# A list scheduler's cost tables: durations and hand-over times by engine pair, and GpSimd and SBUF-to-SBUF VectorE operations apart in the plan

## The chip, the cores and the metric

The kernel runs on one core of a Trainium2 chip. Its time is the device time of one execution in microseconds (us), the median of the runs shown. Five engines work side by side, each through its own list of instructions in order, and wait for one another by semaphores: TensorE (PE, matmuls), VectorE (DVE), ScalarE (ACT), GpSimd (POOL), and SyncE (SP), which issues the DMAs.

## What is computed

The reference is a chain of three transformer layers on 512 tokens of width 1024 in fp32, with 256 tokens of memory. Cut to what matters:

```python
def reference(x, mem, positions, ...):
    mem_n = rmsnorm(mem)
    for i in range(2):                      # first block
        hn = rmsnorm(x)
        mix, q_cross = mla_mixer(hn) if i == 0 else swa_mixer(hn)
        cross = memory_cross_attention(q_cross, mem_n, w_mem_kv[i])
        x = x + concat([mix, cross]) @ w_o[i]
        x = x + squared_relu_mlp(rmsnorm(x), w_up[i], w_down[i])
    x = rmsnorm(x)
    ...                                     # second block, one layer
    a_b, a_c, a_x, q, kc, vc, ksl, vsl, kwn, vwn, g_nsa, g_merge = split(rmsnorm(x) @ w_in)
    y_a = a_b * causal_dwconv(a_c * a_x)
    y_b = nsa(rope(rmsnorm(q)), compressed, selected and window keys and values, gates)
    x = x + (gm_a * (y_a @ w_a_out) + gm_b * (y_b @ w_b_out)) @ w_o
    g, u = split(rmsnorm(x) @ w_ffn_in)
    return x + (silu(causal_dwconv(g) + b) * u) @ w_ffn_out
```

MLA has 12 heads on low-rank queries and keys (`c_q`, `c_kv`, each with a norm of its own, nq and nkv) and a rotated key that all heads share (kr). SWA has 12 heads with a window of 128 tokens, NSA 8 heads with three branches each (compressed, selected, window).

## The kernel before

The activations stay in SBUF transposed, as 8 tiles of 128 features by 512 tokens (`x`). Every dense product is made to fp32 accuracy from three matmuls: a weight chunk (128x512, 256 KB) is loaded by SyncE into one of 4 `raw` buffers, ScalarE rounds it to `h`, and DVE takes the rest, `l = raw - h` (`load_chunk`). For the chunks of the MLA, SWA and first NSA projections GpSimd makes `l` instead (`pool_chunk`). The activation is split in the same way into two `pgr` tiles, and h times both halves and l times the first are summed in PSUM. There are 8 `h` and 8 `l` buffers, and PSUM has 3 banks for dense products (`psd`), 2 for scores (`pss`), 2 for transposes and broadcasts (`pst`) and 1 for values (`pso`). `pgf` are fp32 work tiles of 128x512, `sm` tiles of a few columns.

A norm takes the sums of squares over features with 128x1 matmuls into `pst`, makes the inverse root on DVE with 15 operations on 128x4 elements (`rstd_cols`, `rsqrt`), puts it on the diagonal of four 128x128 blocks, and multiplies these with a matrix of ones on PE, so that every partition has the row; ScalarE copies it to SBUF (`bcast_rows`). The dense products of a normed activation start from x itself, and the row is multiplied in when `psd` is evacuated. n0 is the norm ahead of MLA, nq and nkv are those inside.

The program doesn't run in the order in which it is written. All engine calls are recorded first (`Trace.add`), each as an `Op` with its cost by `_op_cost`, its inputs and its tiles. `Trace.schedule` then makes a plan of the whole kernel: at each step it takes the operation that can start earliest by the plan, and among several on one engine the first by the program's order (with a bias by hand for some groups). An operation can start when its inputs are visible, its engine is free and a buffer is free for each new tile. Visible means the producer's end plus `AFTER` of the producer's engine plus `BEFORE` of the consumer's (`AFTER = {"PE": 197.0, "DVE": 128.0, "ACT": 132.0, "POOL": 75.0, "SP": 2000.0}`). The order in which the plan takes them is the order of each engine's instructions and of the buffers (`emit`); the planned times themselves are used for nothing else. On the chip each engine runs its list as fast as semaphores allow. Since all calls go out from one line of `emit`, that line (L415) stands in every row of the profile, and the names of tiles tell the places apart.

## Time and profile before

| | |
|---|---|
| median of 3 runs | 1916.19 us (1915.88 to 1916.23) |
| span of the profiled execution | 1914.9 us |
| PE busy | 1856.5 us (97%) |
| weight loads of PE | 1527.4 us (80%) |
| DVE busy | 1169.7 us (61%) |
| ACT busy | 835.5 us (44%) |
| POOL busy | 388.9 us (20%) |

The span runs from the first to the last instruction of one profiled execution; the runs' times are 1.3 us longer on the median. A row of the timeline gives start and duration of an instruction (or of several alike in a row, with "x" and their count), the engine, what it writes and reads, and in brackets how long the engine had been idle ahead of it and which engine's result ended that. The durations of matmuls in a row overlap. The clock in the stretches is the share of TensorE's full 2.4 GHz that was granted; 0.5 is its lower level, 1.2 GHz.

In order of time the stages are: memory projections (12 to 43 us), the projections and heads of MLA (to 240), output and MLP (to 640), SWA (to 762), output and MLP (to 1145), the second block's projections and sparse attention (to 1340), and its output and FFN.

### The profile page before, as it was taken

The numbers are of one execution on the slowest core, as the hardware profiler recorded it, in microseconds if no ns is written. First come the engines' busy times: TensorE is split into PE (matmuls) and PEld (weight loads), VectorE is DVE, ScalarE is ACT, GpSimd is POOL, SyncE is SP. The second block draws the span as 40 slices with busy tenths as digits, with TensorE's granted clock in tenths as the row PEclk, the third lists the DMA queues.
The fourth block names the chain that finished last, engine by engine and source line by source line (L and its number), as shares of the span: only waits on it lengthen the run. The fifth ranks groups of instructions, "written<-read, shape, count | busy, mean of one in ns | idle before, by whom it ended". The sixth has DMA issues, their size and how long they took to land.

```text
span 1914.9 us, 25100 instructions
## 1 busy us (share of the span) xinstructions
PE 1856.5 (97%) x8749; PEld 1527.4 (80%) x8749; DVE 1169.7 (61%) x2268; ACT 835.5 (44%) x1674; POOL 388.9 (20%) x431
## 2 busy tenths in 40 slices
PE   6789999999999998999999999999999999999999
PEld 6567688888888876888888887778888888888887
DVE  8588875444446688654444356777755567774652
ACT  7378644332424677443323243447633333332321
POOL 4454320000001354100000040455300122110100
PEclk9899999999999999999999999899999999999999
DMA  6211133333333210333333322311133233333332
GB/s 214 79 49 50 45 94 104 95 99 95 98 99 95 78 56 17 99 105 95 98 98 95 99 81 58 105 45 45 56 94 99 89 93 105 94 99 99 94 99 76
DMA packets 92150, 166.98 MB, mean 87 GB/s; under 512 B 10612, under 2 KB 12408, under 8 KB 92024
## 3 DMA queue, kind: packets, MB, share of 16 engines
q1 hardware_dynamic: 92024, 165.40, 28.8%
q8 instruction: 68, 1.11, 0.2%
q14 instruction: 58, 0.48, 0.1%
HBM read 161.68 MB, written 2.10 MB: 86 GB/s over the span
## 4 chain that ended last, share of the span: by engine, by line
PE 86%; DVE 7%; ACT 3%; issue 2%; POOL 1%; DMA 1%; SPq 0%; DVEq 0%; POOLq 0%; ACTq 0%
PE psd L415 77%; PE pst L415 3%; DVE pgf L415 3%; PE pso L415 3%; PE pss L415 3%; DVE pgr L415 2%; DVE sm L415 1%; ACT pgf L415 1%; ACT pgr L415 1%; POOL pgf L415 1%; DVE l L415 1%; ACT h L415 1%; DMA raw<-w 0%; DVE x L415 0%; DMA pgf<-memT 0%
## 5 line engine op out<-in xcount | busy, mean ns | idle before, releaser
L415 PE MATMUL psd<-pgr,h 128*128 128x512 f32 (+2 forms) x4622 | 1448.8, 393 | 16.2 <-ACT h L415 11.6
L415 PEld LDWEIGHTS psd<-pgr,h 128*128 128x128 f32 (+1 forms) x4622 | 867.4, 189 | 196.0 <-ACT h L415 11.6
L415 PE MATMUL psd<-pgr,l 128*128 128x512 f32 (+2 forms) x2311 | 905.8, 392 | 0.8 <-DVE l L415 0.8
L415 DVE TENSOR_TENSOR l<-raw,h 128x512 fp32r<-128x512 f32 (+1 forms) x536 | 419.4, 785 | 453.9 <-ACT h L415 451.9
L415 ACT CAST h<-raw 128x512 fp32r<-128x512 f32 (+2 forms) x601 | 368.6, 616 | 700.8 <-PE psd L415 618.5
L415 PEld LDWEIGHTS psd<-pgr,l 128*128 128x128 f32 (+1 forms) x2311 | 436.5, 189 | 91.2 <-issue 3.5
L415 POOL TENSOR_TENSOR pgf<-pgf,pgf 128x512 f32<-128x512 f32 (+1 forms) x106 | 142.3, 1345 | 1078.8 <-ACT pgf L415 770.9
L415 DVE TENSOR_TENSOR pgr<-pgf,pgr 128x512 fp32r<-128x512 f32 (+4 forms) x184 | 130.4, 710 | 14.5 <-ACT pgr L415 9.5
L415 ACT CAST pgr<-pgf 128x512 fp32r<-128x512 f32 (+4 forms) x184 | 108.3, 591 | 58.3 <-POOL pgf L415 31.6
L415 ACT ACTIVATE pgf<-pgf 128x512 f32<-128x512 f32 (+2 forms) x125 | 74.9, 602 | 116.4 <-DVE pgf L415 113.2
L415 DVE TENSOR_TENSOR pgf<-psd,pgf 128x512 f32<-128x512 f32 (+2 forms) x102 | 66.9, 657 | 75.3 <-PE psd L415 73.8
L415 POOL TENSOR_TENSOR l<-raw,h 128x512 fp32r<-128x512 f32 (+1 forms) x65 | 88.8, 1377 | 89.5 <-ACT h L415 68.0
L415 PE MATMUL pso<-pgr,pgr 128*128 128x512 f32 (+3 forms) x368 | 90.6, 341 | 4.2 <-DVE pgf L415 1.8
L415 DVE TENSOR_TENSOR pgr<-pst,pgr 128x512 fp32r<-128x512 f32 (+1 forms) x126 | 74.1, 610 | 15.2 <-ACT pgr L415 14.6
L415 POOL TENSOR_SCALAR pgf<-pgf,sm 128x256 f32<-128x256 f32 (+3 forms) x128 | 70.1, 566 | 65.5 <-DVE sm L415 49.6
L415 PE MATMUL pst<-cstt,pgf 128*128 128x128 f32 x436 | 77.7, 277 | 2.6 <-POOL pgf L415 1.5
L415 ACT CAST pgr<-pst 128x512 fp32r<-128x512 f32 (+1 forms) x126 | 63.3, 529 | 28.2 <-PE pst L415 26.8
L415 PE MATMUL pss<-pgr,pgr 128*128 128x256 f32 (+4 forms) x320 | 69.1, 315 | 6.1 <-DVE sm L415 4.0
L415 PEld LDWEIGHTS pso<-pgr,pgr 128*128 128x128 f32 x368 | 58.4, 189 | 19.6 <-ACT pgr L415 7.3
L415 DVE CUSTOM_DVE_ANT_0 pgf<-pss,cmask 128x256 f32<-128x256 f32 (+3 forms) x144 | 65.7, 469 | 12.9 <-PE pss L415 10.8
L415 ACT ACTIVATE pgf<-pgf,sm 128x256 f32<-128x256 f32 (+3 forms) x128 | 65.9, 516 | 16.0 <-DVE sm L415 15.5
L415 PEld LDWEIGHTS pst<-cstt,pgf 128*128 128x128 f32 x436 | 52.7, 140 | 20.5 <-POOL pgf L415 8.3
(115 smaller groups left out, 1122.8 us busy)
## 6 DMA issues: line engine op xcount, KB each, us to landing
raw<-w SPq DMA_DIRECT2D x588, 256.0 KB, 2.6
x<-xT SPq DMA_DIRECT2D x8, 256.0 KB, 5.6
out<-x SPq DMA_DIRECT2D x8, 256.0 KB, 2.0
pgf<-pgf SPq DMA_DIRECT2D x24, 64.0 KB, 2.0
pgf<-aux SPq DMA_DIRECT2D x5, 256.0 KB, 2.7
pgf<-memT SPq DMA_DIRECT2D x4, 256.0 KB, 4.4
raw<-w SPq DMA_DIRECT2D x7, 140.0 KB, 2.1
raw<-w SPq DMA_DIRECT2D x4, 192.0 KB, 2.5
```

The lines of the kernel that those rows point to most:

```text
L415: getattr(getattr(nc, names[o.eng]), o.method)(*[r(x) for x in o.args], **{k: r(v) for k, v in o.kw.items()})
```

## The change

Only the planner changes. The costs in `_op_cost` get other constants (matmuls in fp32r cost their columns plus 32 at 2.4 per ns with a floor of 105 ns, a DMA at least 420 ns of its queue, ScalarE 95 ns more for each operand of one column, a sum taken along costs 75 to 110, and a result of one column on DVE costs 70). The two lists of hand-over times become one table by pair of engines, and 100 ns are added where the result is the operand that PE loads as weights. And in the plan an operation of GpSimd (other than memset), or one of DVE of four kinds that has no PSUM operand, starts only after the last such operation of the other of the two engines has ended. Recorded operations, tiles and their counts stay; their order and the buffers they get may differ.

```diff
--- before.py
+++ after.py
@@ -298,12 +298,30 @@
 
 
 ENGINES = {"tensor": "PE", "vector": "DVE", "scalar": "ACT", "gpsimd": "POOL", "sync": "SP"}
-AFTER = {"PE": 197.0, "DVE": 128.0, "ACT": 132.0, "POOL": 75.0, "SP": 2000.0}
-BEFORE = {"PE": 135.0, "DVE": 0.0, "ACT": 0.0, "POOL": 45.0, "SP": 0.0}
+LAT = {
+    "PE": {"PE": 0.0, "DVE": 211.0, "ACT": 205.0, "POOL": 310.0, "SP": 250.0},
+    "DVE": {"PE": 137.0, "DVE": 126.0, "ACT": 122.0, "POOL": 190.0, "SP": 150.0},
+    "ACT": {"PE": 155.0, "DVE": 140.0, "ACT": 138.0, "POOL": 240.0, "SP": 150.0},
+    "POOL": {"PE": 140.0, "DVE": 150.0, "ACT": 101.0, "POOL": 215.0, "SP": 150.0},
+    "SP": {"PE": 1950.0, "DVE": 1950.0, "ACT": 1950.0, "POOL": 1950.0, "SP": 1950.0},
+}
+LOAD_WEIGHTS = 100.0
+
+
+PORT = ("DVE", "POOL")
+
+
+def _uses_port(o):
+
+    if o.eng == "POOL":
+        return o.method != "memset"
+    if o.eng != "DVE" or any(v.tile.whole for v in o.reads + o.writes):
+        return False
+    return o.method in ("tensor_tensor", "scalar_tensor_tensor", "tensor_scalar", "tensor_copy")
 
 
 class Op:
-    __slots__ = ("i", "eng", "method", "args", "kw", "reads", "writes", "cost", "preds", "succs", "tiles",
+    __slots__ = ("port", "i", "eng", "method", "args", "kw", "reads", "writes", "cost", "preds", "succs", "tiles",
                  "prio", "bias", "npred", "est", "end")
 
 
@@ -318,21 +336,26 @@
     if eng == "PE":
         if method == "transpose":
             return 109.0
-        m, k = _free(args[1]) / 1.2, _free(args[2]) * 0.4167
-        return (max(2 * m, 4 * k) if args[2].dtype == FT else max(m, k)) + 2.5
+        k = _free(args[2])
+        if args[2].dtype == FT:
+            return 2 * max(111.0, (2 * k + 8) / 2.4)
+        return max(105.0, (k + 32) / 2.4)
     if eng == "SP":
-        return 60.0 + n * writes[0].shape[0] * 4 / 340.0
+        return max(420.0, n * writes[0].shape[0] * 4 / 400.0)
+    scalars = [x for x in list(args[2:4]) + [kw.get(k) for k in ("scalar", "bias", "scale")]
+               if isinstance(x, View) and _free(x) == 1]
     if eng == "ACT":
-        return 0.833 * n + (52 if psum else 93) + (220 if accum else 0)
-    scalars = [x for x in list(args[2:4]) + [kw.get("scalar")] if isinstance(x, View) and _free(x) == 1]
+        return 0.833 * n + (52 if psum else 93) + 95 * len(scalars) + (110 if accum else 0)
     if eng == "POOL":
         if method == "memset":
             return 0.833 * n + 60
         if method == "tensor_tensor":
-            return 2.2 * n + 100
-        return 0.833 * n + 160 + 64 * len(scalars)
+            return 2.2 * n + 150
+        return 0.833 * n + 185 + 64 * len(scalars)
     n = max([n] + [_free(v) for v in reads if method == "tensor_reduce"])
-    extra = 68 + (60 if scalars or accum else 0)
+    extra = 68 + (60 if scalars else 0) + (75 if accum else 0)
+    if n == 1:
+        return 70.0
     if method in ("tensor_copy", "tensor_scalar", "memset") and not psum:
         return 0.521 * n + extra
     return 1.042 * n + extra
@@ -403,6 +426,7 @@
         out_costs = writes if writes else [v for v in reads]
         o.cost = _op_cost(eng, method, args, kw, reads, out_costs)
         o.eng = eng
+        o.port = _uses_port(o)
         self.ops.append(o)
 
     def emit(self, tc, order):
@@ -446,6 +470,8 @@
         done = np.zeros(n, bool)
         cur = 0
         engt = {e: 0.0 for e in ENGINES.values()}
+        portt = {e: 0.0 for e in PORT}
+        other = {"DVE": "POOL", "POOL": "DVE"}
         ready = {e: [] for e in engt}
         future = {e: [] for e in engt}
         parked = {}
@@ -483,7 +509,8 @@
                     heapq.heappop(q)
                     offer(o)
                     continue
-                return (engt[e] if r else f[0][0]), o.i
+                at = engt[e] if r else f[0][0]
+                return (max(at, portt[other[e]]) if o.port else at), o.i
 
         for o in ops:
             if o.npred == 0:
@@ -504,15 +531,23 @@
             o.est = st
             o.end = st + o.cost
             engt[e] = o.end
+            if o.port:
+                portt[e] = o.end
             order.append(i)
             done[i] = True
             while cur < n and done[cur]:
                 cur += 1
-            vis = o.end + AFTER[e]
+            lat = LAT[e]
+            vis = o.end + (1950.0 if e == "SP" else 130.0)
             for j in o.succs:
                 s = ops[j]
                 s.npred -= 1
-                s.est = max(s.est, vis + BEFORE[s.eng] if (s.eng != e or e != "PE") else st)
+                if s.eng == "PE" and e != "PE":
+                    own = {id(v.tile) for v in o.writes}
+                    t = o.end + lat["PE"] + (LOAD_WEIGHTS if id(s.args[1].tile) in own else 0.0)
+                else:
+                    t = o.end + lat[s.eng] if (s.eng != e or e != "PE") else st
+                s.est = max(s.est, t)
                 if s.npred == 0:
                     offer(s)
             for t in o.tiles:
```

Three places of the order that follows. Numbers behind a tile's name are buffers.

PE at the broadcast of n0, before (51 to 64 us): `pst` from `ones` is the broadcast, the `psd` rows are MLA's first projections, which read x and weights alone.

```order
L415 MATMUL psd_279<-pgr_318,h_166 128x512
L415 MATMUL psd_279<-pgr_332,h_166 128x512
L415 MATMUL psd_279<-pgr_318,l_178 128x512
L415 MATMUL psd_173<-pgr_318,h_176 128x512
L415 MATMUL pst_359<-pgf_330,ones_72 128x512
L415 MATMUL psd_173<-pgr_332,h_176 128x512
L415 MATMUL psd_173<-pgr_318,l_189 128x512
L415 MATMUL psd_180<-pgr_348,h_191 128x512
L415 MATMUL psd_180<-pgr_361,h_191 128x512
```

The same place after the change.

```order
L439 MATMUL psd_306<-pgr_341,h_273 128x512
L439 MATMUL psd_306<-pgr_492,h_273 128x512
L439 MATMUL psd_306<-pgr_341,l_293 128x512
L439 MATMUL psd_172<-pgr_341,h_282 128x512
L439 MATMUL psd_172<-pgr_492,h_282 128x512
L439 MATMUL psd_172<-pgr_341,l_302 128x512
L439 MATMUL pst_401<-pgf_242,ones_72 128x512
L439 MATMUL psd_179<-pgr_189,h_309 128x512
L439 MATMUL psd_179<-pgr_267,h_309 128x512
```

In the first the broadcast stands in the middle of a chunk, with 38 such matmuls behind it; in the second the three banks are filled first and these 38 stand ahead.

DVE there, before: `sm4_0<-pst_0` is the first operation of n0's chain, rows with 64x256 and 128x512 are splits of the memory's keys and the tables of the rope.

```order
L415 SCALAR_TENSOR_TENSOR pgf_12_149<-pgf_13_157,pgf_12_149 128x512
L415 TENSOR_TENSOR pgr_33_468<-pgf_8_117,pgr_33_468 64x256
L415 SCALAR_TENSOR_TENSOR pgf_12_149<-pgf_13_157,pgf_12_149 128x512
L415 TENSOR_TENSOR pgr_33_468<-pgf_8_117,pgr_33_468 64x256
L415 TENSOR_SCALAR pgf_12_149<-pgf_12_149 128x512
L415 TENSOR_TENSOR pgr_34_478<-pgf_8_117,pgr_34_478 64x256 x2
L415 TENSOR_SCALAR sm4_0_584<-pst_0_196 128x4
L415 TENSOR_TENSOR pgr_35_497<-pgf_8_117,pgr_35_497 64x256
L415 TENSOR_SCALAR sm4_1_591<-sm4_0_584 128x4
L415 TENSOR_TENSOR pgr_35_497<-pgf_8_117,pgr_35_497 64x256
L415 TENSOR_SCALAR sm4_2_596<-sm4_1_591 128x4
```

After the change.

```order
L439 TENSOR_TENSOR pgf_12_150<-psd_2_306,pgf_4_90 128x256
L439 SCALAR_TENSOR_TENSOR pgr_38_492<-x7_16_191,vecs_1_74,pgr_26_341 128x512
L439 CAST pgf_13_159<-pgf_15_198 128x512
L439 TENSOR_TENSOR pgf_12_150<-psd_0_172,pgf_4_90 128x256
L439 TENSOR_SCALAR sm4_0_608<-pst_0_208 128x4
L439 TENSOR_SCALAR pgf_13_159<-pgf_13_159,cstt_2_100 128x512
L439 TENSOR_SCALAR sm4_1_614<-sm4_0_608 128x4
L439 TENSOR_TENSOR pgr_32_434<-pgf_11_143,pgr_32_434 64x256
L439 TENSOR_SCALAR sm4_2_635<-sm4_1_614 128x4
L439 TENSOR_SCALAR pgf_6_102<-pgf_13_159 128x512
L439 TENSOR_TENSOR sm4_1_614<-sm4_2_635 128x4
```

The chain's first operation moved from row 72 of DVE's list to row 60, behind the last evacuation (`psd`) of the memory's keys.

DVE at the broadcast of nkv, before (95 to 105 us): the rows of `sm4_10` and `sm4_11` are the end of nkv's chain, the rows with `cstt_2` the diagonal, 128x512 rows the normed `c_q`, 64x512 and 32x512 the rope of kr.

```order
L415 SCALAR_TENSOR_TENSOR pgr_42_886<-pgf_2_84,vecs_1_74,pgr_40_875 128x512
L415 SCALAR_TENSOR_TENSOR pgr_44_894<-pgf_3_88,vecs_1_74,pgr_41_884 128x512
L415 SCALAR_TENSOR_TENSOR pgr_45_899<-pgf_5_96,vecs_1_74,pgr_43_891 128x512
L415 TENSOR_TENSOR sm4_10_851<-sm4_11_854 128x4
L415 TENSOR_TENSOR pgf_13_157<-psd_0_173,pgf_19_346 64x512
L415 TENSOR_TENSOR sm4_10_851<-sm4_10_851,sm4_9_848 128x4
L415 TENSOR_TENSOR pgf_9_123<-pgf_13_157,pgf_16_309 32x512
L415 TENSOR_SCALAR sm4_10_851<-sm4_10_851 128x4
L415 TENSOR_TENSOR pgf_18_344<-pgf_13_157,pgf_15_234 32x512
L415 TENSOR_TENSOR sm4_11_854<-sm4_11_854,sm4_10_851 128x4
L415 TENSOR_TENSOR pgf_9_123<-pgf_9_123,pgf_18_344 32x512
L415 TENSOR_SCALAR pgf_8_117<-cstt_2_104,sm4_11_854 128x128 x4
```

After the change.

```order
L439 TENSOR_SCALAR sm4_10_841<-sm4_10_841 128x4
L439 TENSOR_TENSOR sm4_11_845<-sm4_11_845,sm4_10_841 128x4
L439 TENSOR_TENSOR pgf_2_84<-pgf_2_84,pgf_14_195 128x512
L439 TENSOR_TENSOR pgf_7_110<-pgf_7_110,pgf_14_195 128x512
L439 TENSOR_TENSOR pgf_3_88<-pgf_3_88,pgf_14_195 128x512
L439 SCALAR_TENSOR_TENSOR pgr_42_902<-pgf_2_84,vecs_1_74,pgr_40_892 128x512
L439 SCALAR_TENSOR_TENSOR pgr_44_909<-pgf_7_110,vecs_1_74,pgr_41_898 128x512
L439 SCALAR_TENSOR_TENSOR pgr_45_915<-pgf_3_88,vecs_1_74,pgr_43_905 128x512
L439 TENSOR_SCALAR pgf_4_90<-cstt_2_100,sm4_11_845 128x128 x4
L439 TENSOR_TENSOR pgf_8_119<-psd_0_172,pgf_10_134 64x512
L439 TENSOR_TENSOR pgf_19_242<-psd_1_179,pgf_10_134 128x512
L439 TENSOR_TENSOR pgf_13_159<-pgf_8_119,pgf_18_225 32x512
```

The end of the chain moved ahead of the six rows of `c_q`, and the diagonal ahead of the rope's.

ScalarE in the query tiles of the sparse attention, before (1208 to 1216 us): a tile is scaled (`vecs`) and squared out of the same `psd`; the casts of 64x512 split a tile of an earlier step.

```order
L415 CAST h_6_268<-raw_0_115 128x512
L415 ACTIVATE pgf_12_149<-psd_2_279,vecs_1_74 128x512
L415 CAST pgr_47_947<-pgf_3_88 64x512
L415 CAST pgr_46_944<-pgf_3_88 64x512
L415 ACTIVATE pgf_2_84<-psd_2_279 128x512
L415 CAST h_2_176<-raw_2_139 128x512
L415 CAST h_3_191<-raw_3_151 128x512
```

After the change.

```order
L439 CAST h_0_163<-raw_3_130 128x512
L439 CAST h_5_282<-raw_0_108 128x512
L439 ACTIVATE pgf_7_110<-psd_0_172,vecs_1_74 128x512
L439 ACTIVATE pgf_8_119<-psd_0_172 128x512
L439 CAST h_6_309<-raw_1_116 128x512
L439 CAST h_2_175<-raw_2_123 128x512
L439 CAST pgr_8_139<-pgf_13_159 64x512
L439 CAST pgr_3_112<-pgf_13_159 64x512
L439 CAST h_3_184<-raw_3_130 128x512
```

Scale and square of a tile now stand together ahead of the two casts.

## Rows read from the trace of the kernel before

**Rows 1.** The page: busy time, share of the span and instructions of each engine.

```profile
PE 1856.5 (97%) x8749; PEld 1527.4 (80%) x8749; DVE 1169.7 (61%) x2268; ACT 835.5 (44%) x1674; POOL 388.9 (20%) x431
```

**Rows 2.** Stretches: us; each engine's busy us (instructions); clock; DMA share and GB/s.

```profile
105.00:240.00 135.00, 129.01 (x672) 98.93 (x673) 114.47 (x305) 103.94 (x261) 59.48 (x89) 1.00 0.15 46
250.00:600.00 350.00, 350.00 (x1547) 289.56 (x1546) 170.26 (x268) 126.88 (x218) 9.76 (x8) 1.00 0.33 99
640.00:762.00 122.00, 112.94 (x643) 91.96 (x642) 95.90 (x260) 90.18 (x240) 63.34 (x96) 1.00 0.17 51
1145.00:1270.00 125.00, 115.78 (x591) 94.57 (x589) 90.13 (x253) 50.67 (x106) 40.31 (x33) 0.92 0.26 74
```

**Rows 3.** PE's timeline at n0's broadcast: start, us, operation, [idle before and releaser].

```profile
63.22 2.08 PE L415 MATMUL pst<-pgf,ones 128*128 128x512 f32 x2 [11.52 <-DVE pgf L415]
74.27 0.62 PE L415 MATMUL psd<-pgr,h 128*128 128x512 f32 x2
```

**Rows 4.** The same view: DVE, GpSimd and ScalarE around it.

```profile
48.66 0.16 DVE L415 TENSOR_SCALAR sm<-pst 128x4 f32<-128x4 f32 x1
...
51.96 1.22 DVE L415 TENSOR_TENSOR sm<-sm,sm 128x4 f32<-128x4 f32 x1
...
59.28 0.15 DVE L415 TENSOR_TENSOR sm<-sm,sm 128x4 f32<-128x4 f32 x1
...
62.29 0.87 DVE L415 TENSOR_SCALAR pgf<-cstt,sm 128x128 f32<-128x128 f32 x4
73.21 2.02 DVE L415 TENSOR_TENSOR pgf<-psd,pgf 128x512 f32<-128x512 f32 x3 [10.05 <-PE psd L415]
39.79 6.63 POOL L415 TENSOR_TENSOR l<-raw,h 128x512 fp32r<-128x512 f32 x4 [5.07 <-ACT h L415]
50.47 8.61 POOL L415 TENSOR_TENSOR l<-raw,h 128x512 fp32r<-128x512 f32 x6 [4.05 <-ACT h L415]
65.33 0.59 ACT L415 COPY pgf<-pst 128x512 f32<-128x512 f32 x1 [8.90 <-PE pst L415]
```

**Rows 5.** The same view, SyncE's DMA queue, and the stretch of the memory projections.

```profile
5.85 1.03 SPq L415 DMA_DIRECT2D x<-xT  x2
12.95 2.67 SPq L415 DMA_DIRECT2D raw<-w  x4
11.60:26.00 14.40, 12.59 (x76) 12.07 (x76) 13.94 (x29) 10.11 (x18) 5.78 (x5) 1.00 0.69 216
```

**Rows 6.** The same view: PE at the broadcast of nkv, then DVE.

```profile
105.34 1.13 PE L415 MATMUL pst<-pgf,ones 128*128 128x512 f32 x2 [3.34 <-DVE pgf L415]
98.55 1.25 DVE L415 TENSOR_TENSOR sm<-sm 128x4 f32<-128x4 f32 x1
99.73 0.67 DVE L415 TENSOR_TENSOR pgf<-psd,pgf 64x512 f32<-64x512 f32 x1
...
103.28 2.01 DVE L415 TENSOR_SCALAR pgf<-cstt,sm 128x128 f32<-128x128 f32 x4
```

**Rows 7.** The same view: PE at the end of SWA's heads, then two stretches.

```profile
748.30 0.35 PE L415 MATMUL pso<-pgr,pgr 128*128 128x256 f32 x1 [0.96 <-DVE pgf L415]
...
752.21 0.38 PE L415 MATMUL pso<-pgr,pgr 128*128 128x256 f32 x1 [1.57 <-DVE sm L415]
744.00:753.00 9.00, 5.90 (x41) 4.89 (x41) 8.87 (x26) 7.61 (x23) 3.82 (x9) 1.00 0.00 0
1291.00:1301.00 10.00, 10.00 (x63) 8.27 (x63) 8.81 (x24) 6.11 (x15) 6.05 (x5) 1.00 0.27 80
```

**Rows 8.** PE's waits from 1130 to 1330 (total, times, longest); then PE and ScalarE.

```profile
PE pso L415 <- ACT pgf L415: 3.6, 2, 2.9
PE pss L415 <- DVE pgr L415: 2.0, 1, 2.0
1214.94 1.05 PE L415 MATMUL pso<-cstt,pgf 128*128 128x2 f32 x8 [2.92 <-ACT pgf L415]
1213.01 1.26 ACT L415 CAST pgr<-pgf 64x512 fp32r<-64x512 f32 x2 [2.21 <-DVE pgf L415]
```

## The prediction

> **What bounds the kernel now.** I read the page first, then the time by stretches, then PE's waits and the timeline where they lie. The page says that PE is busy 97% of the span and the next engine, VectorE (DVE), 61% [rows 1]. The stretches say where the other 3% are: in the long dense stretch from 250 to 600 us PE is busy 350.00 of 350.00 us, 0.226 us for each of 1547 matmuls [rows 2]. No order of the same matmuls can shorten that, and there the change leaves PE's order as it is. What an order can win lies in the attention stages and the start: 6.0 us of PE's time idle from 105 to 240 us, 9.1 from 640 to 762, 9.2 from 1145 to 1270, where the granted clock is also 0.92 on the mean [rows 2], and two single waits at the start, 11.52 us for DVE's `pgf` at the broadcast of the norm n0 [rows 3] and 3.34 us at that of nkv [rows 6]. So the change is worth what it takes from these waits, less what its new order loses elsewhere. Nothing in the work itself is added or removed.
>
> **The broadcast of n0.** In the trace of before PE stands idle 11.52 us and starts the `pst` matmul of the broadcast at 63.22; behind it come 38 `psd` matmuls that need nothing of the norm, and PE is through with them at 74.27 [rows 3]. The norm's chain on DVE, 15 tiny operations and four for the diagonal, runs from 48.66 to 63.16 [rows 4], though one of its operations takes 0.15 us when nothing disturbs it (59.28) and 1.22 us while GpSimd is in its row of `l<-raw,h` (51.96, inside 50.47 to 59.08) [rows 4]. The changed order does two things. On PE it puts all 38 matmuls ahead of the broadcast; at 0.226 us they are 8.6 us of work for the hole that begins at 51.70, so PE has it filled to 60.3. On DVE the chain begins 12 rows earlier in the row, with as many other operations mixed into it as before. Until the chain is done PE still waits: I put the broadcast at 62 to 64, because GpSimd, which in before idles 4.05 us ahead of its second row (50.47), has its ten operations, 15.2 us of them [rows 4], beside this chain. After the broadcast PE has nothing to do until a PSUM bank is free: 1.13 us for the two matmuls at full clock [rows 6], 0.59 us for ScalarE's copy and a third of 2.02 us for the first evacuation [rows 4], with the hand-overs between them some 2.8 us by estimate. That makes 65 to 67 where before had 74.27, a gain of 7 to 9 us. I take **7**, because the last of the 38 need an `l` that GpSimd delivered only at 59.08. Ends: 4 if GpSimd's first row (6.63 us, four operations) also falls on the chain, which by the 1.07 us between the two durations above is 4.3 us more; 9 if it doesn't.
>
> One rule speaks against the way in which the plan counts on this. The Trainium skill, SBUF — State Buffer, section "Who interferes with whom", says that GpSimd and a VectorE operation with two SBUF inputs take the shared port pair as an exclusive lock for a whole instruction, and that the order of issue decides who blocks. The 1.22 us against 0.15 us agrees with that. By this rule a plan that keeps the two apart on paper holds only as long as the engines keep to its times, since no semaphore is added; if they slip, n0 gives 4 us and the sum is -6.4 in place of -9.4. The second rival below is this, carried on.
>
> **The loads at the start.** SyncE now issues six tiles of x, the positions and a table ahead of the fifth and later weight chunks. In before its queue has nothing between 6.88 and 12.95, when the raw buffers are full [rows 5], so much of this moves into a hole. At the 216 GB/s of that stretch the six tiles, the positions and the table (256 KB each) take 9.7 us of transfer and end near 16.6, 3.6 us after the time at which the next weights began to load. So the cost is between 0 and 3.6 us; PE is busy 12.59 of 14.40 us there and DVE 13.94 [rows 5], so little slack hides it, but tiles loaded early needn't be loaded later. ScalarE's evacuation of a memory projection also goes behind two weight casts. I take **+2**.
>
> **The broadcast of nkv.** PE waits 3.34 us at 105.34. On DVE the end of the chain is mixed with four operations for the rope of kr (from 99.73, 0.67 us the first) and the diagonal comes at 103.28 [rows 6]. In the changed order the chain of nkv is done before the six large operations of nq, and the diagonal comes right behind these, ahead of the four. In before the large ones end at 98.55 [rows 6]; the nine small operations now ahead of them cost 9 x 0.2 = 1.8 us at the most, so the diagonal starts near 100.4, 2.9 earlier. The four rope operations are late by as much, but they are not waited for at once (the shared key is needed when the first head's scores start). I take **-3**, between 0 and the whole 3.34.
>
> **The heads of MLA and SWA.** Here several hundred rows change places by a few positions, and no wait stands out. MLA I take at 0, within 3 either way, half of the 6.0 us idle. In SWA the end is bound by DVE: 8.87 busy of 9.00 us while PE has 5.90 [rows 7]. The changed order has two stretches without a single `psd` matmul between the heads' own, of 40 and 26 rows, where before has one of 33; and ScalarE's table load for the next rope moves earlier into the same tail. 33 more rows at 5.90/41 = 0.144 us are 4.8 us of work, and at the pace of that tail (9.00/5.90) they would leave 2.5 us idle. Against that some of the 9.1 us idle may go. I take **0**, within 4.
>
> **The sparse attention.** Of its waits two are named: 2.9 us for ScalarE's `pgf` at 1214.94 and 2.0 us for DVE's `pgr` [rows 8]. The first comes from ScalarE's order: the two casts at 1213.01, which had waited 2.21 us for DVE, stand ahead of the Square that PE needs [rows 8]. The changed order has scale and Square of that tile ahead of those casts, and the score matmuls of the second wait stand among more `psd` work. So -4.9. But that work is taken from later: the new order has one stretch of 69 matmuls, scores, transposes and values, without a `psd` matmul among them, where before has none over 25 rows in this block. At 10.00/63 = 0.159 us they are 11.0 us of work. From below the cost is 0, since from 1291 to 1301 attention with a few fillers kept PE at 10.00 of 10.00 us, with DVE at 8.81 [rows 7]; from above it is SWA's tail, 11.0 x (9.00/5.90 - 1) = 5.8. DVE's 8.81 with the fillers taken away is nearer to the tail, so I take +3.5. Together **-1.4**, between -4.9 and +5.8.
>
> **The sum.** -7 + 2 - 3 + 0 + 0 - 1.4 = -9.4 us. The profiled execution has a span of 1914.9 us, 1.3 under the median of the runs, 1916.19; the difference is taken from the median: 1906.8, say **1907**.
>
> **Rivals.** (1) The forecast, 1900 to 1912. (2) The separation isn't kept and gains slide on: the engines leave the plan's times early, GpSimd's ten operations fall on the chain of n0 (-4), the loads cost their 3.6, nkv's 3.34 comes back at the next wait because DVE has the same sum of work, and the sparse attention is even. That gives 1916. For it: DVE is busy 114.47 of 135 us from 105 to 240 [rows 2]. Against it: 38 matmuls that wait for nothing are moved into the hole whatever GpSimd does. (3) Slower: the heads run short of filler. Between the two waits at 748.30 and 752.21 are 3.91 us with 1.57 of them idle [rows 7], a ratio of 1.67. At that ratio the 11.0 us of the sparse attention lose 7.4 and SWA's 4.8 lose 3.2; and after idle time PE runs at half clock, as the 2.08 us for two matmuls at 63.22 [rows 3] against 1.13 at 105.34 [rows 6] show: on half of the 11.0 us that is 5.5 more. 16.1 against the -8 of the start, with nothing won from the two named waits, gives 1924. It decides from a loss of 11.8 us in these stretches. Against it: full PE from 1291 to 1301. (4) More: the loads cost nothing (-2), SWA and the sparse attention have their waits without new ones (-4 and -3.5), and n0 is -9: 1895.
>
> **How the numbers follow.** What a measurement of this kernel can tell from no change is about 0.2%, 3.8 us: faster is under 1912.4, slower over 1920.0. Chances: forecast 0.50, even 0.15, slower 0.15, more 0.20. So faster 0.70, same 0.15, slower 0.15. The range reaches from 1892, somewhat beyond the fourth case, to 1921, past the second into the third: both ends are about a tenth.
>
> **What would show it.** In the trace of after PE's wait at the broadcast of n0 should be under 4 us, with the 38 matmuls ahead of it, and a second wait of 2 to 4 us behind it for a PSUM bank. At nkv the wait should be under 1 us. If the small operations there still take 1.2 us throughout, the second case is at work. Around 1215 the wait for ScalarE should be gone; if in the block's heads a stretch without `psd` has DVE at 9.5 of 10 us, PE under 7 and a clock under 0.9, the third is. The dense stretches should not change; if they do, all of this is wrong.

## The result, and the profile after

The changed kernel takes **1927.94 us** (median of 4 runs, 1927.35 to 1929.94), where the runs of before beside it gave 1916.04. The ratio is 1.0066, with a 95% interval of 1.0052 to 1.0080: slower by two thirds of a percent, where the prediction had 1907 and at most 1921. The page of after has the same counts of instructions, and 12 us more on TensorE (PE); its first line:

```profile
PE 1868.4 (97%) x8749; PEld 1537.2 (80%) x8749; DVE 1164.0 (60%) x2268; ACT 837.1 (43%) x1674; POOL 387.1 (20%) x431
```

PE is busy 11.9 us longer than in [rows 1] for the same 8749 instructions, and VectorE (DVE) 5.7 us shorter. The span grew by 11.0 us. So summed over the kernel the loss is time in which PE worked: the waits that went and the waits that came make up for each other. Where it arose shows best along PE's own work. Below, k is a count of PE's matmuls and transposes in order of their start (a matmul in plain fp32 leaves two records in the profile and is counted once), and the table compares the times at which the two kernels start their k-th; the last line ends at the last of them.

| stretch of k | stage | before, us | after less before, us | forecast |
|---|---|---|---|---|
| to 200 | memory projections | 44.0 | +8.8 | +2 |
| 200 to 400 | broadcasts of n0 and nkv | 65.5 | -9.0 | -7 and -3 |
| 400 to 1000 | heads of MLA | 127.5 | 0.0 | 0 |
| 1000 to 2750 | output, MLP | 397.6 | +1.7 | 0 |
| 2750 to 3500 | SWA | 143.8 | +11.8 | 0 |
| 3500 to 5100 | output, MLP | 363.4 | 0.0 | 0 |
| 5100 to 5600 | projections of the sparse attention | 120.9 | -6.4 | -4.9 |
| 5600 to 6300 | its heads | 129.8 | +4.0 | +3.5 |
| 6300 to the end | output, FFN | 518.4 | +0.1 | 0 |

Seven of the nine sums are near the forecast, though not all by the way that was forecast (see below). The two others are 6.8 and 11.8 us over it, 18.6 of the 21 us by which the time was missed.

**The memory projections.** By stretches (each engine's busy us, instructions, granted clock, DMA share, GB/s), before:

```profile
11.60:20.00 8.40, 8.33 (x42) 8.01 (x43) 8.04 (x18) 6.58 (x12) 3.11 (x3) 1.00 0.59 191
20.00:28.00 8.00, 6.08 (x49) 5.83 (x48) 7.84 (x17) 5.53 (x11) 3.26 (x3) 1.00 0.86 268
28.00:36.00 8.00, 7.78 (x64) 7.47 (x62) 8.00 (x9) 7.91 (x18) 5.89 (x4) 1.00 0.60 196
```

and after:

```profile
11.60:20.00 8.40, 7.16 (x39) 6.84 (x40) 7.84 (x11) 8.40 (x17) 6.14 (x6) 1.00 1.01 370
20.00:28.00 8.00, 4.42 (x33) 3.81 (x32) 8.00 (x11) 6.10 (x11) 6.57 (x4) 1.00 0.22 67
28.00:36.00 8.00, 4.61 (x23) 4.32 (x23) 5.44 (x16) 2.74 (x6) 0.00 (x0) 0.51 0.63 200
```

The early loads of x fill the DMA engines: 370 GB/s at a share of 1.01 up to 20 us, where before had 191 at 0.59. Then PE is busy 4.42 of 8 us and 4.61 of 8, the second at half clock. Rows of after from GpSimd, DVE, ScalarE and PE (start, duration, operation, idle ahead and releaser):

```profile
16.05 10.75 POOL L439 TENSOR_TENSOR pgf<-pgf,pgf 128x512 f32<-128x512 f32 x6 [1.95 <-ACT pgf L439]
...
25.61 1.21 DVE L439 TENSOR_TENSOR sm<-sm 128x2 f32<-128x2 f32 x1
...
32.51 0.47 ACT L439 ACTIVATE pgf<-psd,sm 128x256 f32<-128x256 f32 x1 [0.91 <-DVE sm L439]
27.47 0.38 PE L439 MATMUL psd<-l,pgr 128*128 128x256 f32 x1 [2.58 <-DVE l L439]
...
33.03 0.58 PE L439 MATMUL psd<-h,pgr 128*128 128x256 f32 x1 [3.39 <-ACT pgf L439]
```

Since x is there early, ScalarE and GpSimd work on its squares at once: GpSimd adds up six of them without a break from 16.05 to 26.80. Beside them an operation of 128x2 elements in the chain of the memory's norm takes 1.21 us; six of the chain's small operations take over 1 us, where in before two did. The chain is late (its last small operation ends at 32.38, in before at 25.56), ScalarE's evacuation waits for its `sm` at 32.51, all three `psd` banks are full until then, and PE waits 3.39 us. The 2.58 us at 27.47 are an `l` whose weights landed late. By PE's records up to the 200th matmul, 6.3 of the 8.8 us are idle time and 2.5 longer work.

**The broadcasts.** At n0, after:

```profile
68.95 1.02 PE L439 MATMUL pst<-pgf,ones 128*128 128x512 f32 x2
75.20 1.22 PE L439 MATMUL psd<-pgr,h 128*128 128x512 f32 x2 [5.24 <-DVE pgf L439]
61.75 1.25 DVE L439 TENSOR_TENSOR sm<-sm 128x4 f32<-128x4 f32 x1
...
67.57 0.87 DVE L439 TENSOR_SCALAR pgf<-cstt,sm 128x128 f32<-128x128 f32 x4
...
72.74 1.48 DVE L439 TENSOR_SCALAR pgf<-pgf 128x512 f32<-128x512 f32 x1
...
74.47 0.68 DVE L439 TENSOR_TENSOR pgf<-psd,pgf 128x512 f32<-128x512 f32 x1
61.50 1.48 POOL L439 TENSOR_TENSOR l<-raw,h 128x512 fp32r<-128x512 f32 x1 [0.75 <-ACT h L439]
68.24 1.28 ACT L439 ACT_TABLE_LOAD   x1
...
71.62 0.57 ACT L439 COPY pgf<-pst 128x512 f32<-128x512 f32 x1
```

The answer to [rows 3] is that the wait of 11.52 us is gone: PE goes from the last of the 38 matmuls straight into the broadcast. But PE came 8.8 us late, and the diagonal was made at 68.44, just ahead of it, 5.3 us later than in before: the late start hid the end of the chain (f4 below starts on time, and waits 5.29 us there). The wait for a PSUM bank that the prediction put behind it is there, with 5.24 us in place of 1.7 (2.8 less 1.1 for the broadcast itself; its signs allowed 2 to 4), because ScalarE has a table load, sine, cosine and two casts ahead of the copy (71.62), and DVE rope operations, two of them 1.5 us each beside GpSimd, ahead of the first evacuation (74.47). PE is at 75.20 where before had it at 74.27, so of its 8.8 us it has made up 7.9. At nkv the answer to [rows 6] is a wait of 1.51 us for 3.34, where the prediction's sign was under 1:

```profile
104.25 1.10 PE L439 MATMUL pst<-pgf,ones 128*128 128x512 f32 x2 [1.51 <-DVE pgf L439]
```

**SWA.** The stage in two parts, before:

```profile
634.70:713.70 79.00, 78.02 (x453) 65.69 (x451) 58.09 (x154) 56.78 (x148) 41.01 (x58) 1.00 0.22 64
713.70:778.50 64.80, 56.71 (x301) 44.97 (x302) 56.44 (x132) 46.59 (x117) 27.05 (x43) 0.97 0.14 41
```

and after:

```profile
636.20:718.90 82.70, 79.75 (x452) 66.19 (x450) 57.66 (x154) 57.40 (x149) 38.69 (x58) 0.99 0.22 65
718.90:791.90 73.00, 63.90 (x301) 51.27 (x302) 55.89 (x132) 46.31 (x116) 24.88 (x43) 0.84 0.11 34
```

PE stood 9.1 us in before (1.0 and 8.1) and 12.0 in after (2.9 and 9.1), 3.0 more before rounding. The same work, 754 and 753 instructions, kept it busy 134.7 us and 143.7, 8.9 more, at a clock of 0.84 in the second part where before had 0.97. So three quarters of SWA's loss are time at the slower clock: in after's four stretches at half clock PE was busy 21.5 us, which at full clock would by estimate be 10.7 less, where before had 3.4 and 1.7. This says where the time went; no run has this order at full clock throughout, where PE might have waited more for the engines that feed it. PE's rows where the clock fell, before's row for the last of them, and ScalarE's rows at the end:

```profile
715.99 0.91 PE L439 MATMUL pss<-pgr,pgr 128*128 128x128 f32 x4 [1.17 <-DVE sm L439]
...
732.02 0.69 PE L439 MATMUL pss<-pgr,pgr 128*128 128x128 f32 x2 [1.92 <-DVE sm L439]
...
773.42 2.08 PE L439 MATMUL psd<-pgr,h 128*128 128x512 f32 x4 [3.64 <-ACT pgr L439]
761.03 1.23 PE L415 MATMUL psd<-pgr,h 128*128 128x512 f32 x4 [2.04 <-ACT pgr L415]
770.41 1.28 ACT L439 ACT_TABLE_LOAD   x1
771.71 1.15 ACT L439 ACTIVATE pgf<-pgf 128x512 f32<-128x512 f32 x2
```

PE ran at half clock behind the row at 715.99, the longest of three short waits, and again around the one at 732.02, which stands at the end of the shorter of the two new stretches without `psd`; the row at 773.42 is at half clock itself (2.08 us for four matmuls, against 1.23 for four at 761.03 in before). Ahead of the last one ScalarE loads the table for the next rope (1.28 us) and makes sine and cosine (1.15) before it casts what PE waits for.

**The sparse attention.** In the projections the answer to [rows 8] is 0.77 us in place of 2.92. In the heads the stretch of 69 matmuls without `psd` takes from 1283.6 to 1302.3, 18.7 us, where the prediction had 11.0 of work and 3.5 of waits: PE waits 2.6 us and works 16.2, more than half of the stretch at half clock:

```profile
1220.30 1.05 PE L439 MATMUL pso<-cstt,pgf 128*128 128x2 f32 x8 [0.77 <-ACT pgf L439]
...
1286.45 0.44 PE L439 MATMUL pss<-pgr,pgr 128*128 128x128 f32 x2 [1.68 <-DVE sm L439]
1283.59:1302.32 18.73, 16.17 (x71) 12.44 (x70) 13.88 (x58) 11.38 (x30) 4.78 (x8) 0.73 0.05 15
1287.00:1299.00 12.00, 11.38 (x42) 8.98 (x42) 7.81 (x36) 7.51 (x21) 4.78 (x8) 0.57 0.01 2
```

The whole stage of the projections (k from 5100 to 5600), before and after:

```profile
1141.80:1262.70 120.90, 112.54 (x577) 92.73 (x576) 85.24 (x238) 48.22 (x98) 37.18 (x31) 0.92 0.27 77
1155.30:1269.80 114.50, 109.97 (x577) 90.67 (x576) 76.36 (x214) 48.19 (x98) 39.63 (x33) 0.97 0.27 80
```

PE stands 8.4 us in before and 4.5 in after, 3.8 less; the other 2.6 of the 6.4 us are shorter work at a higher clock, and that can also come from run to run (last section).

### The profile page after: what moved, and what is told of

Same layout as the page of the kernel before. It is cut to its first block, busy times and chain, and to the rows that moved or that the text cites. A ratio compares the mean times of both kernels' runs of the same rounds, so it can differ in the third digit from the quotient of the medians.

```text
span 1926.0 us, 25046 instructions
## 1 busy us (share of the span) xinstructions
PE 1868.4 (97%) x8749; PEld 1537.2 (80%) x8749; DVE 1164.0 (60%) x2268; ACT 837.1 (43%) x1674; POOL 387.1 (20%) x431
## 4 chain that ended last, share of the span: by engine, by line
PE 91%; DVE 4%; ACT 2%; DMA 1%; issue 1%; SPq 0%; POOL 0%; ACTq 0%; DVEq 0%; POOLq 0%
PE psd L439 81%; PE pst L439 4%; PE pss L439 3%; PE pso L439 3%; DVE pgf L439 2%; ACT pgf L439 1%; DVE pgr L439 1%; DVE sm L439 1%; DMA raw<-w 0%; ACT pgr L439 0%; DMA x<-xT 0%; SPq L439 0%; DMA pgf<-memT 0%; DMA pgf<-posr 0%; POOL pgf L439 0%
## 5 line engine op out<-in xcount | busy, mean ns | idle before, releaser
L439 PE MATMUL psd<-pgr,h 128*128 128x512 f32 (+2 forms) x4622 | 1448.8, 393 | 25.6 <-ACT h L439 12.2
L439 PEld LDWEIGHTS psd<-pgr,h 128*128 128x128 f32 (+1 forms) x4622 | 866.6, 189 | 204.6 <-ACT h L439 12.2
L439 DVE TENSOR_TENSOR l<-raw,h 128x512 fp32r<-128x512 f32 (+1 forms) x536 | 413.6, 774 | 459.8 <-ACT h L439 459.0
L439 POOL TENSOR_TENSOR pgf<-pgf,pgf 128x512 f32<-128x512 f32 (+1 forms) x106 | 143.7, 1359 | 1060.1 <-ACT pgf L439 755.2
L439 PEld LDWEIGHTS pss<-pgr,pgr 128*128 128x128 f32 x320 | 54.7, 202 | 18.8 <-DVE sm L439 10.0
```

The costliest lines, as they stand in the source:

```text
L439: getattr(getattr(nc, names[o.eng]), o.method)(*[r(x) for x in o.args], **{k: r(v) for k, v in o.kw.items()})
```

## The experiments

Every kernel computes all of the reference; only the plan differs. Stages are told from the profiled execution of each kernel, against the one of before; a single profile can hold a stretch of half clock more or less (last section), so a difference under 4 us in one stage of one profile is not read by itself. Times are medians with the range of the runs.

**Is it the loads, at the start?** e1 puts the early loads alone into the kernel before, e2 takes them alone out of the changed one.

```diff
     if eng == "SP":
+        if writes[0].tile.name.startswith("x"):
+            return 60.0
         return 60.0 + n * writes[0].shape[0] * 4 / 340.0
```

> The kernel before, with one cost changed in its plan: the eight loads of x cost 60 ns of SyncE's time in place of 831, so that x2 to x7, the positions and the table go out ahead of the fifth weight chunk, as in the changed kernel; the order of all else stays nearly that of before. Theory L (the loss at the start comes from these loads): TensorE's 200th matmul, at 44.0 us in before and 52.8 in after, comes at 50 to 53, TensorE waits for l and for the memory's evacuation between 22 and 33 us, and it runs at half clock there; the wait at the broadcast of n0 takes some of it back, so the time is 1918 to 1924. Rival O (the loss comes from the new order on ScalarE and VectorE in the memory stage): the 200th matmul stays within 2 us of 44.0 and the time within 2 us of 1916.

Measured: 1918.86 us (1916.09 to 1920.00), ratio 1.0019 (1.0009 to 1.0030). The time is in theory L's range, the 200th matmul, at 49.0 and 5.0 late, just short of it; n0's broadcast takes nothing of this back (+0.1), the heads of MLA 1.8. The first stretch's DMA and PE's wait for the memory's evacuation are like those of after; ScalarE's row shows weights that came late:

```profile
11.60:20.00 8.40, 8.31 (x46) 8.00 (x47) 7.53 (x15) 4.99 (x10) 3.13 (x3) 1.00 1.00 368
31.69 0.58 PE L417 MATMUL psd<-h,pgr 128*128 128x256 f32 x1 [3.59 <-ACT pgf L417]
19.43 0.62 ACT L417 CAST h<-raw 128x512 fp32r<-128x512 f32 x1 [3.41 <-DMA raw<-w]
```

GpSimd's six squares in a row are not there, its longest row is 3.04 us, and four of the chain's operations are slow. So the row of six comes from the early loads and after's order on ScalarE together, and the loads alone cost by late weights too: ScalarE stands 3.41 us for a chunk whose load went out behind x.

e2, against the changed kernel:

```diff
+        at = {"x2": 16e3, "x3": 16.2e3, "x4": 20e3, ..., "posr": 27e3, "aux": 28e3, "sel": 33e3}
+        for o in ops:
+            if o.eng == "SP" and o.writes:
+                o.est = at.get(o.writes[0].tile.name.split("_")[0], 0.0)
```

> The changed kernel with one thing taken back: in the plan the loads of x2 to x7, the positions and the tables are not released before the times at which the kernel before issued them. The new costs, hand-over times and the rule on the shared port stay, and SWA and the sparse attention have exactly the order of after. Theory L: the 200th matmul comes back to 44 to 46 us from 52.8, and the gains at n0 and nkv (10 us from the 100th to the 400th matmul in after) stay for the most part, so the time is 1928 less 5 to 9: 1919 to 1923. Rival O: the 200th matmul stays at 50 or later, 1926 to 1930.

Measured: 1920.79 us (1920.16 to 1924.21), ratio 1.0036 (1.0020 to 1.0052), 7 under the changed kernel and in theory L's range. The 200th matmul is 3.3 late in place of 8.8 (theory L had 0 to 2), and the gain at n0 and nkv stays (-8.6). DMA is back to 155 GB/s, but one wait remains:

```profile
11.60:20.00 8.40, 7.21 (x31) 6.89 (x32) 7.85 (x15) 5.87 (x11) 3.60 (x4) 1.00 0.54 155
29.75 0.39 PE L439 MATMUL psd<-h,pgr 128*128 128x256 f32 x1 [3.98 <-ACT pgf L439]
```

So the loads make 5 to 6 us of the 8.8. The rest is by subtraction rival O's: in the new order more other operations stand among the chain of the memory's norm, which ends at 27.89 where before had 25.56, and ScalarE has two tiles of x to split and square, the first waiting for its DMA, ahead of the evacuation, which starts at 29.24 for 25.66.

**Does SWA lose by its own order?** e3 plans operations 4190 to 5739 by the old rules, e4 the memory stage (0 to 319) too. The planner then gives SWA word for word the order of before.

```diff
+OLD = [(0, 320), (4190, 5740)]      # e3: the second alone
+def _old(o):
+    return any(a <= o.i < b for a, b in OLD)
...
-        o.cost = _op_cost(eng, method, args, kw, reads, out_costs)
+        o.cost = (_op_cost_before if _old(o) else _op_cost)(eng, method, args, kw, reads, out_costs)
-        o.port = _uses_port(o)
+        o.port = _uses_port(o) and not _old(o)
...
+                if _old(o):
+                    t = vis + BEFORE[s.eng] if (s.eng != e or e != "PE") else st
```

> The changed kernel, but the operations of the second layer's SWA stage (and these alone) are planned with the old costs and hand-over times and without the rule on the port; its order there is then exactly that of before, all other stages keep the order of after. Theory S (the 11.8 us that SWA loses are made by its own new order): 1928 less 10 to 13, 1915 to 1918, half clock in SWA back from 24 us to under 7. Rival D (the stage loses by what it is handed: prefetched weights, buffers, the clock's phase): 1924 to 1930.

Measured: 1915.64 us (1912.24 to 1921.38), ratio 1.0004 (0.9992 to 1.0017). SWA is 1.2 us shorter than before's in place of 11.8 longer; the start still loses 7.5. Rival D is out: what the stage is handed costs nothing that this profile shows.

> As the run before, and the memory stage with the loads of x is planned by the old rules too (operations 0 to 319 and 4190 to 5739); n0, MLA and the sparse attention by the new ones. If the losses are local and add up: 1928 - 11.8 - 7 = 1909, with 3 either way, under the kernel before. If n0's gain in after was only the other side of the late memory stage (its broadcast had to wait less because all else came later): 1914 to 1917. Rival D: 1920 or more.

Measured: 1911.63 us (1906.29 to 1913.58), ratio 0.9973 (0.9962 to 0.9984): faster than before. The 200th matmul is 0.6 us early, and n0 and nkv still give 6.5. So most of their gain was not the other side of the late start, but 2.5 of its 9.0 us were; with this the two losses add up (1927.9 - 11.8 - 8.8 + 2.5 = 1909.8 by the profiles).

**Which part of the change makes SWA's loss?** f1 to f3 are e4 with one part of the change switched on in SWA, the other two off.

```diff
-        o.port = _uses_port(o) and not _old(o)
+        o.port = _uses_port(o) and o.i >= 320                         # f1
-        o.cost = (_op_cost_before if _old(o) else _op_cost)(...)
+        o.cost = (_op_cost_before if _old(o) and o.i < 320 else _op_cost)(...)   # f2
-                if _old(o):
+                if _old(o) and o.i < 320:                             # f3
```

> As e4_start_swa_old (1911.6 us), but in SWA the rule on the shared port is on, with the old costs and hand-over times. Theory P (the rule on the port makes SWA's loss): SWA, from TensorE's 2750th to 3500th matmul, is 8 to 12 us longer than before's 143.8 us, half clock there over 15 us, time 1920 to 1924. Rival C (the durations do, costs and hand-over times): within 3 us of 143.8, time 1910 to 1915.

Measured: 1911.38 us (1909.55 to 1916.67), ratio 0.9984 (0.9973 to 0.9996). In the profiled run, one of the longer ones at 1916.19, SWA takes 5.2 us more than before's.

> As e4_start_swa_old, but in SWA the costs are the new ones, with the old hand-over times and without the rule on the port. Theory P: SWA within 3 us of 143.8 us, time 1910 to 1915. Rival C: 5 to 12 us longer, if the costs carry it; under 5 in both this and the next run would mean that the parts lose only together.

Measured: 1915.59 us (1913.84 to 1921.76), ratio 1.0003 (0.9991 to 1.0015). SWA takes 5.4 us more.

> As e4_start_swa_old, but in SWA the hand-over times are the new ones, with the old costs and without the rule on the port. Theory P: SWA within 3 us of 143.8 us, time 1910 to 1915. Rival C: 5 to 12 us longer, if the hand-over times carry it.

Measured: 1910.93 us (1909.34 to 1912.95), ratio 0.9975 (0.9965 to 0.9985). SWA takes 1.6 us more.

Neither theory holds: no single part gives 11.8. By the profiles they add up to 12.2, by the medians only the costs cost anything for certain (4 us over e4). The half clock in SWA is 20.5 us with the port rule, 6.8 with the costs and 13.7 with the hand-over times, against 3.4 in before, so it doesn't go in step with the loss, and in f2 PE works 3.8 us longer than in before, more than twice what the clock there makes by the estimate above. The shares are not settled. But one piece of the mechanism has an owner. PE's waits at the end of SWA (total, times, longest), with the port rule alone:

```profile
PE psd L475 <- ACT pgr L475: 4.3, 2, 3.7
```

and with the costs alone:

```profile
PE psd L475 <- ACT pgr L475: 2.1, 1, 2.1
```

The 3.6 us wait of after is there with the port rule, and 2.1 with the costs or the hand-over times alone.

**The table load in SWA's tail.** h1 and h2 move the 13 operations of the second block's rope tables out of SWA, in the changed kernel and in the one before; h3 does it in f4.

```diff
+        for o in ops:
+            if o.writes and o.writes[0].tile.name.startswith("r64"):
+                o.est = 900e3
```

> The changed kernel; in its plan the 13 operations that make the second block's rope tables (11 on VectorE, two on ScalarE with a table load) are not released before 900 us, so that they go from SWA's tail into the dense stretch behind it. The order of SWA is otherwise that of after. Theory T (the table load ahead of the last cast): TensorE's wait of 3.6 us at the end of SWA falls to about 2.0 and the half clock behind it goes; SWA loses 5 to 8 us where after lost 11.8, time 1921 to 1925. Rival H (the heads' order): SWA still loses 10 us or more, 1926 to 1930; and if the eleven VectorE operations were all of it, under 3.

Measured: 1923.31 us (1922.56 to 1924.67), ratio 1.0039 (1.0023 to 1.0055), 4.6 under the changed kernel. SWA loses 8.0 in place of 11.8, and the last wait is 2.1:

```profile
PE psd L439 <- ACT pgr L439: 2.4, 2, 2.1
768.41 2.08 PE L439 MATMUL psd<-pgr,h 128*128 128x512 f32 x4 [2.08 <-ACT pgr L439]
```

So about a third of the loss goes with the 13 operations; that it is the table load among them, and not the eleven on DVE, is argued from the rows above and not shown. The other part of theory T failed: the half clock didn't go. PE's row behind the wait is still at half clock (2.08 us for four matmuls), and SWA has 20.5 us of it for 23.9; of the 8.0 us left, 0.5 are idle time. Two thirds remain with the order of the heads. DVE's waits for ScalarE's casts in SWA are longer in that order, before and after:

```profile
DVE pgr L415 <- ACT pgr L415: 6.5, 9, 1.8
```

```profile
DVE pgr L439 <- ACT pgr L439: 10.9, 14, 1.8
```

Both engines work in order; in the changed order DVE stands more often before a split whose cast isn't done, and all that is behind it in its list waits too. This fits the waits of PE for DVE's `sm`; no run takes these waits alone away.

> The kernel before with the same release of the rope tables. By theory T its SWA stage, too, gets shorter, by 1 to 4 us, since its tail is bound by VectorE: waits of 1.57 at 752.21 and 2.04 at 761.03 go down; 1912 to 1915. By rival H it stays within 1 us of 143.8, at 1914 to 1918.

Measured: 1913.57 us (1910.00 to 1916.02), ratio 0.9986 (0.9976 to 0.9996). SWA is 1.7 us shorter, under what one profile can tell; the whole kernel is 2.7 us shorter by the medians.

**A version that beats both.** f4 is e4 with the heads of the sparse attention by the old rules as well:

```diff
-OLD = [(0, 320), (4190, 5740)]
+OLD = [(0, 320), (4190, 5740), (8660, 10000)]
```

> As e4_start_swa_old, and the operations 8660 to 9999 (heads of the sparse attention and the work around them) are planned by the old rules too, so that its matmuls have before's order there; new rules remain for n0, MLA and the projections ahead of those heads. Theory F (the stretch of 69 matmuls without filler costs 3 to 4 us net): the step from the 5600th to the 6300th matmul goes from +3.8 to within 1 of before's 129.8 us, time 3 to 4 us under e4: 1907 to 1909. Rival N (the filler put early gives the gain of the projections and the two cancel): the projections' gain, 3.4 us from the 5100th to the 5600th in e4, goes as well, and the time stays at 1911 to 1913.

Measured: **1906.13 us** (1905.51 to 1908.39), ratio 0.9949 (0.9933 to 0.9966). The heads go from +3.8 to -0.4, no stretch without `psd` is over 24 matmuls there, and the projections keep their -3.6, so the filler theory holds; the order of the heads comes near to before's without being it. That the time is the 1907 of the forecast is chance: n0 and nkv give 5.1 where 10 were forecast, and the projections' 3.6 are no more than before's own order gave in e1 and h2. PE's rows at n0 and nkv, and the page's first line:

```profile
64.80 2.08 PE L475 MATMUL pst<-pgf,ones 128*128 128x512 f32 x2 [5.29 <-DVE pgf L475]
68.35 1.22 PE L475 MATMUL psd<-pgr,h 128*128 128x512 f32 x2 [1.47 <-DVE pgf L475]
98.22 1.10 PE L475 MATMUL pst<-pgf,ones 128*128 128x512 f32 x2 [1.50 <-DVE pgf L475]
PE 1858.2 (97%) x8749; PEld 1529.5 (80%) x8749; DVE 1169.6 (61%) x2268; ACT 835.9 (44%) x1674; POOL 390.3 (20%) x431
```

With the start on time the broadcast of n0 still waits 5.29 us and starts at 64.80, later than in before (63.22): eight of the chain's small operations take 1.1 to 1.3 us beside GpSimd. What is won is the work done ahead of it: PE takes up `psd` again at 68.35 for 74.27.

> f4_only_early_gains (1906.1 us) with the same release. Theory T: as much less as in h2, 1902 to 1905. Rival H: 1905 to 1908.

Measured: 1906.85 us (1905.90 to 1907.62), ratio 0.9951 (0.9935 to 0.9968): no better than f4.

**Is it luck?** A greedy planner could turn any small change of numbers into a new order. g1 and g2 vary the costs of the kernel before by up to 3%, g3 and g4 those of the changed one.

```diff
         o.cost = _op_cost(eng, method, args, kw, reads, out_costs)
+        o.cost *= 0.97 + 0.0006 * (o.i * 7919 % 101)      # g2, g4: 6007
```

> The kernel before; in its plan the cost of each operation is multiplied by a number between 0.97 and 1.03 that depends on its place in the program alone (7919 times it, modulo 101). Theory R (what the change did to the stages is due to its new numbers and rule): no stage moves by more than 3 us, the time is within 4 us of 1915.7. Rival L (any small change of the plan's numbers reorders the attention stages, and what comes out there is luck): some attention stage moves by 4 us or more. The order of SWA is nearly that of before here, so SWA should not move by either; the projections of the sparse attention are reordered.

Measured: 1911.46 us (1910.16 to 1914.57), ratio 0.9975 (0.9964 to 0.9986). SWA 0.0; the projections of the sparse attention -6.0.

> The same with another series (6007 in place of 7919). Here SWA's order differs from that of before by as much as one of the change's parts makes (8.7 places on the mean). Theory R: SWA within 3 us of before's 143.8, time within 4 us of 1915.7. Rival L: SWA moves by 4 us or more, either way.

Measured: 1917.10 us (1914.23 to 1918.31), ratio 1.0002 (0.9990 to 1.0013). SWA -0.7, though its order changed as much as by one part of the change.

> The changed kernel with its costs varied by up to 3% in the same way (7919). SWA's order stays near that of after (1.2 places on the mean). Theory R: 1928 with 4 either way, SWA again 8 to 12 us over before, the start again 7 to 10 us late at the 100th matmul. Rival L: SWA's loss is under 6 or over 15 us, or the time is under 1922.

Measured: 1926.06 us (1923.87 to 1931.13), ratio 1.0054 (1.0019 to 1.0088). Start +8.6, n0 and nkv -8.4, SWA +9.4, projections -6.3.

> The same with 6007. Theory R: as the run before, 1928 with 4 either way. Rival L: under 1922, or SWA's loss under 6 or over 15 us.

Measured: 1932.92 us (1930.29 to 1936.13), ratio 1.0088 (1.0063 to 1.0114). Start +8.5, n0 and nkv -9.0, SWA +13.2, projections -6.7, heads +5.5; the time is 0.9 us above theory R's range.

So the loss at the start, the gain at the broadcasts and the loss in SWA belong to the new numbers: in two draws they come out again under other costs, and don't come out of jitter on the old ones (for SWA that is g2 alone, as g1 hardly changes its order). The gain in the projections belongs to them only in part: jitter alone gave -6.0, with a gain of about 5 us for the whole kernel, and e1 and h2, with before's own order there, had -3.8, all of it by a higher clock (PE idle 8.5 and 8.7 us for before's 8.4). PE's idle time there does fall more under the new numbers: by 3.8 us in after, by 1.0 and 2.2 in g1 and g2.

## Why the prediction was wrong

- **What bounds the kernel: right, but for the clock.** It looked for gains and losses in waits of PE. The dense stretches did stay as they were (+0.0 and +0.1; the +1.7 in the first MLP goes with 3.4 us at half clock at its very start, from 239.8 to 243.2). But waits were only 3.0 of the 11.8 us that SWA lost.
- **n0 and nkv: right in the mechanism, and in size by luck.** -10 forecast, -9.0 measured; but -8.4 to -9.4 come only where the start is late and PE arrives when most of the chain is done. With the start on time it is -5.1 to -6.5 (e4, f1 to f4, h3): n0 gives 4.7 in f4 for the 7 forecast (5.9, less the 1.2 by which f4 is early ahead of it), inside its bounds, and at both places more wait is left than the signs allowed (5.29 for under 4, 1.50 for under 1). That the chain would lie beside GpSimd was right too: DVE's operation at 61.75 takes 1.25 us where others take 0.16, and ends with GpSimd's of 61.50. The Trainium skill's rule that the order of issue decides (SBUF — State Buffer, section "Who interferes with whom") agrees with that trace: GpSimd's began first, and DVE's was done when it was. The plan keeps the two engines apart, the chip doesn't. DVE's busy time fell by 5.7 of 1169.7 us.
- **The loads: the term that was mis-sized,** +2 with bounds of 0 and 3.6, measured +8.8. The bound was a sum of bytes by the rate of the DMA engines. It left out that weights behind them land late enough for ScalarE and PE to wait (e1), what the tiles set going once they are there (GpSimd's squares, 10.75 us in a row beside the norm's chain, ScalarE's splits ahead of its evacuation), and the half clock behind PE's waits. "Tiles loaded early needn't be loaded later" brought no gain that shows: early work took the engines from the chain that PE waited for. e1 and e2 show 5 to 6 us of it; with the whole stage by the old rules it is gone (e4).
- **SWA: the step that failed,** 0 within 4, measured +11.8. The prediction saw both pieces, the stretches without `psd` and the table load, and set a possible gain from the idle time against them. It priced the new stretches by idle time alone (2.5 us; 3.0 measured in the stage) and left out the slower clock (8.9), which it had priced only in the third rival, and for the sparse attention. That the stage's own order makes the loss is shown (e3); how much of it each of the two pieces and each part of the change makes is not, beyond the third that goes with the rope tables (h1).
- **The sparse attention: right in sum, by luck in part** (-1.4 forecast, -2.4 measured). The stretch without filler cost what it was put at (f4: from +3.8 to -0.4), but not as idle time alone: of the heads' 4.0 us 2.3 are idle and 1.7 longer work, with 10.2 us at half clock where before had none: the term that was left out in SWA. In the projections the idle time fell by 3.8 for the 4.9 forecast; the rest of the -6.4 goes with a higher clock, such as e1 and h2 have it with before's order.
- **The rivals.** The second, that the separation isn't kept, is what the trace shows; at n0 it kept the broadcast from coming earlier (64.80 in f4), but the work moved ahead was won all the same. The third had the right mechanism, heads short of filler and then half clock, with a total of 16.1 us; in the sparse attention it came true in part (in the stretch the clock is 0.73, its sign was under 0.9, but PE is busy 16.2 of 18.7 us and DVE 13.9), and in SWA, for which it had 3.2, the loss was 11.8, part of it behind waits that it didn't name; "nothing won from the two named waits" was wrong. The range to 1921 left out that two terms could miss in the same direction.

## What to carry to other kernels

A better cost table is worth measuring stage by stage: here it won 9 us in one stage and lost 21 in two others and the sum hid both, and planning the losing stages by the old rules gave a kernel 0.5% under the one before and 1.1% under the changed one. Half of such a gain can be chance: 3% of jitter on the old costs gave 0.25% (g1). Price a new wait of TensorE with the half clock behind it, which cost three times the added waits in SWA. And price an early transfer by the work that it releases on other engines and by the loads behind it, not by its bytes alone.

## What the runs showed of the hardware

- After waits of 1.17 us and less (715.99 and the two behind it) PE's clock was granted at half, 1.2 GHz, from 717.6 on; PE was busy 7.99 of the 10 us from 710 to 720:

```profile
710.00:720.00 10.00, 7.99 (x45) 5.88 (x44) 7.22 (x22) 7.95 (x25) 3.25 (x7) 0.88 0.15 50
```

  In SWA of after this happened four times, for 23.9 us in all, against 3.4 in before; h1 had 20.5.
- The length of the last wait alone doesn't tell the clock. Behind a wait of 2.1 us at the end of SWA, the same four matmuls took 2.08 us in h1 (768.41) and 1.22 in f2 (764.47).
- The half clock comes and goes from run to run in the same order. Runs of before spread from 1912.1 to 1918.6 us; e1 and h2, with before's order in the second block's projections, have 13.7 us of half clock there where before's profile had 20.5, and are 3.8 us shorter there. A gain of less than that in one stage of one profile shows nothing.
- A table load of ScalarE takes 1.28 us, and the next activation starts 1.30 us after it (770.41 and 771.71). The Trainium skill, ScalarE: Activation LUTs, section "What ACT_TABLE_LOAD costs", gives the same for the load and, for a switch to another set of tables, 1.38 us more for a drain; the rows show no such time, neither behind it nor ahead of it (the operation before ends at 770.39).
